# A batched matmul, scheduled by Tile or written engine by engine with its own semaphores

## The chip, the cores and the metric

The kernel runs on one core of one Trainium2 chip. The metric is the device time of one execution in microseconds (us).

The profile lists the instructions of five engines. In the kernel before, PE multiplies (768 matmuls, 189.9 us busy), DVE (VectorE) casts (48 casts, 83.1 us), ACT (ScalarE) empties the accumulators (64 copies, 64.9 us), SP (SyncE) issues the transfers (49 of them), and POOL (GpSimd) does nothing of note (0.2 us). The transfers stand in one queue, whose packets take 98.5% of the time of the 16 DMA engines that the page counts.

## The reference

```python
batch, m, k, n = 16, 512, 768, 1024
x: (batch, k, m) float32      y: (batch, k, n) float32
out = einsum('bkm,bkn->bmn', x, y)      # (16, 512, 1024) float32
```

Per batch 1.57 MB of x and 3.15 MB of y are read and 2.10 MB are written: 6.82 MB, of which nothing can be spared.

## The kernel before

It is written in Tile: pools of rotating buffers, and Tile places every wait. Three things matter here: the order in which SP issues transfers, the two rotating buffers of each input, and the last y, which comes in two halves.

```python
    xs_pool = ctx.enter_context(tc.tile_pool(name="xs_pool", bufs=2))
    ys_pool = ctx.enter_context(tc.tile_pool(name="ys_pool", bufs=2))
    ...
    o_pool = ctx.enter_context(tc.tile_pool(name="o_pool", bufs=5))
    LAG = 4
    ...
        for b in range(B):
            ...
            halves = 2 if b == B - 1 else 1
            nc.sync.dma_start(xs[:], x_v[b])
            for h in range(halves):
                ks = slice(h * KT // halves, (h + 1) * KT // halves)
                nc.sync.dma_start(ys[:, ks], y_v[b, :, ks])
            if b >= LAG:
                store(b - LAG)
            ...
            nc.vector.tensor_copy(x_sb[:], xs[:])
            for h in range(2):
                ks = slice(h * KH, (h + 1) * KH)
                nc.vector.tensor_copy(y_sb[:, ks], ys[:, ks])
            ...
            for h in range(halves):
                for mo in range(MT):
                    ...   # 6 matmuls for each of two accumulator halves
                    if h == halves - 1:
                        nc.scalar.copy(o_sb[:, mo]..., ps[mo][:])
        for b in sorted(o_tiles):
            store(b)
```

The store of a batch is issued four batches after its loads (`LAG`), so that in the end four older stores stand in the queue behind the last y.

Of the kernel before, what the change touches and what calls it, by code (L numbers as in the profile page):

```python
# [1 line left out]

_os.environ.setdefault("NEURON_RT_ULTRASERVER_MODE", "4")

# [1 line left out]

# [4 lines left out]


@with_exitstack
def kernel(
    ctx: ExitStack,
    tc: tile.TileContext,
    x: bass.AP,
    y: bass.AP,
    out: bass.AP,
):  # L20
    nc = tc.nc
    P = 128
    FP32 = mybir.dt.float32
    BF16 = mybir.dt.bfloat16

    B, K, M = x.shape
    _, _, N = y.shape
    KT = K // P
    MT = M // P
    NF = 512  # L30
    NT = N // NF



    x_v = x.rearrange("b (p ko) m -> b p ko m", ko=KT)
    y_v = y.rearrange("b (p ko) n -> b p ko n", ko=KT)
    o_v = out.rearrange("b (p mo) n -> b p mo n", mo=MT)

    xs_pool = ctx.enter_context(tc.tile_pool(name="xs_pool", bufs=2))
    ys_pool = ctx.enter_context(tc.tile_pool(name="ys_pool", bufs=2))  # L40
    x_pool = ctx.enter_context(tc.tile_pool(name="x_pool", bufs=2))
    y_pool = ctx.enter_context(tc.tile_pool(name="y_pool", bufs=2))
    o_pool = ctx.enter_context(tc.tile_pool(name="o_pool", bufs=5))
    psum = ctx.enter_context(tc.tile_pool(name="psum", bufs=4, space=bass.MemoryType.PSUM))
    LAG = 4
    KH = KT // 2
    o_tiles = {}

    def store(b):
        o_sb = o_tiles.pop(b)  # L50

        nc.sync.dma_start(o_v[b], o_sb[:])

    with tc.manual_schedule():
        for b in range(B):
            xs = xs_pool.tile([P, KT, M], FP32, name="xs")
            ys = ys_pool.tile([P, KT, N], FP32, name="ys")
            halves = 2 if b == B - 1 else 1
            nc.sync.dma_start(xs[:], x_v[b])  # L59
            for h in range(halves):  # L60
                ks = slice(h * KT // halves, (h + 1) * KT // halves)
                nc.sync.dma_start(ys[:, ks], y_v[b, :, ks])
            if b >= LAG:
                store(b - LAG)
            x_sb = x_pool.tile([P, KT, M], BF16, name="x_sb")
            y_sb = y_pool.tile([P, KT, N], BF16, name="y_sb")
            nc.vector.tensor_copy(x_sb[:], xs[:])  # L67
            for h in range(2):
                ks = slice(h * KH, (h + 1) * KH)
                nc.vector.tensor_copy(y_sb[:, ks], ys[:, ks])  # L70
            x_w = x_sb[:].rearrange("p k (j mo) -> p k mo j", mo=MT)
            o_sb = o_pool.tile([P, MT, N], FP32, name="o_sb")
            o_tiles[b] = o_sb
            ps = {}


            for h in range(halves):
                for mo in range(MT):
                    if h == 0:
                        ps[mo] = psum.tile([P, NT, NF], FP32, name="ps")  # L80
                    for nt in range(NT):
                        for kt in range(h * KT // halves, (h + 1) * KT // halves):
                            nc.tensor.matmul(  # L83
                                ps[mo][:, nt], x_w[:, kt, mo],
                                y_sb[:, kt, nt * NF:(nt + 1) * NF],
                                start=(kt == 0), stop=(kt == KT - 1))
                    if h == halves - 1:
                        nc.scalar.copy(o_sb[:, mo].rearrange("p (t f) -> p t f", f=NF), ps[mo][:])  # L88
        for b in sorted(o_tiles):
            store(b)  # L90


# [1 line left out]
_INS = ['x', 'y']  # L94
_OUTS = [((16, 512, 1024), 'float32')]


# [23 lines left out]
```

## Time and profile before

| | before |
|---|---|
| time, median of the runs | 262.0 us (261.9 to 262.17) |
| span of the profile | 260.4 us |
| rate over the span | 419 GB/s |
| first load issued | 0.73 us |
| last store issued | 246.03 us |

The main lines of the page and of the timeline are in the prediction below. The page's list of transfers (what it writes and reads, the issuing queue, how many, size, median time from issue to landing):

```profile
ys<-in_y_dram SPq DMA_DIRECT2D x15, 3072.0 KB, 28.1
...
xs<-in_x_dram SPq DMA_DIRECT2D x16, 1536.0 KB, 29.7
```

1.57 MB take 29.7 us to land, where 428 GB/s would need 3.7: so most of those 29.7 us are spent behind other transfers. The view of the line that closes the program (minimum, median and maximum duration in ns, then start of the first and of the last such instruction):

```profile
L116 SPq DRAIN  x3: 7/7/7, 259.7 to 260.0; - x3
...
L116 PEldq EVENT_SEMAPHORE  x2: 51/51/51, 259.9 to 260.4; - x2
```

When the last store has landed, SP joins two rounds of "all engines are done", at 259.7 and 260.0, and PE's answer to the second one, at 260.4, ends the span. This is the frame of the program; it costs 0.7 us after the last landing.

### The profile page before, as it was taken

The numbers are of one execution on the slowest core, as the hardware profiler recorded it, in microseconds if no ns is written. First come the engines' busy times: TensorE is split into PE (matmuls) and PEld (weight loads), VectorE is DVE, ScalarE is ACT, GpSimd is POOL, SyncE is SP. The second block draws the span as 40 slices with busy tenths as digits, with TensorE's granted clock in tenths as the row PEclk, the third lists the DMA queues.
The fourth block names the chain that finished last, engine by engine and source line by source line (L and its number), as shares of the span: only waits on it lengthen the run. The fifth ranks groups of instructions, "written<-read, shape, count | busy, mean of one in ns | idle before, by whom it ended". The sixth has DMA issues, their size and how long they took to land.

```text
span 260.4 us, 1815 instructions
## 1 busy us (share of the span) xinstructions
PE 189.9 (73%) x768; PEld 89.1 (34%) x768; DVE 83.1 (32%) x48; ACT 66.2 (25%) x65; POOL 0.2 (0%) x4
## 2 busy tenths in 40 slices
PE   0049999897939949598495956939789597899600
PEld 0014555453513514244142422514325233355200
DVE  0271734525222252322524214252132522252000
ACT  1003343433321313314033330412404114131600
POOL 0000000000000000000000000000000000000000
PEclk9999999999986997979899997997959869799955
DMA  7999999999999999999999999999999999999995
GB/s 276 430 427 425 451 420 436 423 386 421 439 428 430 422 433 445 418 435 422 435 436 414 452 405 448 429 415 452 413 434 426 421 447 416 427 437 422 428 435 214
DMA packets 7065, 109.18 MB, mean 419 GB/s; under 512 B 784, under 2 KB 784, under 8 KB 784
## 3 DMA queue, kind: packets, MB, share of 16 engines
q1 hardware_dynamic: 7056, 109.06, 98.5%
q8 instruction: 6, 0.10, 0.1%
q14 instruction: 3, 0.02, 0.0%
HBM read 75.50 MB, written 33.55 MB: 419 GB/s over the span
## 4 chain that ended last, share of the span: by engine, by line
DMA 74%; DVE 11%; PE 8%; ACT 0%; issue 0%; SPq 0%; DVEq 0%
DMA ys<-in_y_dram 74%; DVE y_sb L70 11%; PE ps L83 8%; ACT o_sb L88 0%; SPq L59 0%; DVEq L70 0%
## 5 line engine op out<-in xcount | busy, mean ns | idle before, releaser
L83 PE MATMUL ps<-y_sb,x_sb 128*128 128x512 bf16 x768 | 189.9, 410 | 55.1 <-DVE y_sb L70 55.1
L83 PEld LDWEIGHTS <-x_sb 128*128 128x128 bf16 x768 | 89.1, 118 | 155.3 <-issue 44.6
L88 ACT COPY o_sb<-ps 128x1024 f32<-128x1024 f32 x64 | 64.9, 1014 | 179.1 <-PE ps L83 179.1
L70 DVE CAST y_sb<-ys 128x3072 bf16<-128x3072 f32 x32 | 55.0, 1757 | 87.6 <-DMA ys<-in_y_dram 87.6
L67 DVE CAST x_sb<-xs 128x3072 bf16<-128x3072 f32 x16 | 28.2, 1760 | 66.4 <-DMA xs<-in_x_dram 65.6
L88 ACT ACT_TABLE_LOAD x1 | 1.3, 1283 | 0.7 <-PEq L105 0.7
L105 POOL MEMSET const-bfloat16-1.0<- 128x1 bf16 x1 | 0.1, 101 | 0.0
L105 POOL MEMSET const-uint8-127<- 128x1 uint8 x1 | 0.1, 101 | 0.0
L105 POOL MEMSET const-float32-0.0<- 128x1 f32 x1 | 0.1, 98 | 0.2 <-issue 0.2
L105 POOL MEMSET const-float32-1.0<- 128x1 f32 x1 | 0.1, 98 | 0.0
## 6 DMA issues: line engine op xcount, KB each, us to landing
ys<-in_y_dram SPq DMA_DIRECT2D x15, 3072.0 KB, 28.1
out_dram<-o_sb SPq DMA_DIRECT2D x16, 2048.0 KB, 32.6
xs<-in_x_dram SPq DMA_DIRECT2D x16, 1536.0 KB, 29.7
ys<-in_y_dram SPq DMA_DIRECT2D x2, 1536.0 KB, 26.1
```

The costliest lines, as they stand in the source:

```text
L67: nc.vector.tensor_copy(x_sb[:], xs[:])
L70: nc.vector.tensor_copy(y_sb[:, ks], ys[:, ks])
L83: nc.tensor.matmul(ps[mo][:, nt], x_w[:, kt, mo], y_sb[:, kt, nt * NF:(nt + 1) * NF], start=(kt == 0), stop=(kt == KT - 1))
L88: nc.scalar.copy(o_sb[:, mo].rearrange("p (t f) -> p t f", f=NF), ps[mo][:])
L105: nc = _bacc.Bacc("TRN2", target_bir_lowering=False, num_devices=1)
```

## The change

The intent: the same order of work, but with each engine's program written out by hand and with semaphores of its own, in the hope that fewer and cheaper waits than Tile's give a faster kernel. It is not quite the same order: the two waits in front of a batch's loads (for the x cast, and for the y casts) are joined into one, and the halves of the last y are gone. Tile's context still stands around it (`tile_critical`, and a `Block` inside). The core of the diff, cuts marked:

```diff
-    xs_pool = ctx.enter_context(tc.tile_pool(name="xs_pool", bufs=2))
... (all pools go)
+    ctx.enter_context(tc.tile_critical())
... (buffers, one semaphore for each input and output buffer)
+    cast = ec(nc.semaphore("cast"))
+    ready = ec(nc.semaphore("ready"))
+    room = ec(nc.semaphore("room"))
+    groups = ec(nc.semaphore("groups"))
+    outs = ec(nc.semaphore("outs"))
+    block = ec(nc.Block())
+    @block.sync
+    def _(sync):
+        def store(b):
+            sync.wait_ge(outs, b + 1)
+            sync.dma_start(o_v[b], ob[b % NO][:]).then_inc(so[b % NO], 16)
         for b in range(B):
-            halves = 2 if b == B - 1 else 1
-            nc.sync.dma_start(xs[:], x_v[b])
-            for h in range(halves):
-                ks = slice(h * KT // halves, (h + 1) * KT // halves)
-                nc.sync.dma_start(ys[:, ks], y_v[b, :, ks])
+            i = b % 2
+            if b >= 2:
+                sync.wait_ge(cast, b - 1)
+            sync.dma_start(xs[i][:], x_v[b]).then_inc(sx[i], 16)
+            sync.dma_start(ys[i][:], y_v[b]).then_inc(sy[i], 16)
             if b >= LAG:
                 store(b - LAG)
...
+            nc.vector.tensor_copy(xb[i][:], xs[i][:]).then_inc(ready, 1)
...
+            vector.drain().then_inc(cast, 1)
+    def batch(tensor, i, first):
+        tensor.wait_ge(ready, 2).then_inc(ready, -2)
+        for mo in range(MT):
+            tensor.wait_ge(room, 1).then_inc(room, -1)
...
+                    if mo == 0 and nt == 0 and kt == KH:
+                        tensor.wait_ge(ready, 1).then_inc(ready, -1)
```

More of the change, by code (lines that the diff above doesn't have):

```diff
@@ L37 @@
     o_v = out.rearrange("b (p mo) n -> b p mo n", mo=MT)
-    xs_pool = ctx.enter_context(tc.tile_pool(name="xs_pool", bufs=2))
-    ys_pool = ctx.enter_context(tc.tile_pool(name="ys_pool", bufs=2))
-    x_pool = ctx.enter_context(tc.tile_pool(name="x_pool", bufs=2))
-    y_pool = ctx.enter_context(tc.tile_pool(name="y_pool", bufs=2))
-    o_pool = ctx.enter_context(tc.tile_pool(name="o_pool", bufs=5))
-    psum = ctx.enter_context(tc.tile_pool(name="psum", bufs=4, space=bass.MemoryType.PSUM))
@@ L45 @@
     LAG = 4
+    NO = 5
     KH = KT // 2
-    o_tiles = {}
-    def store(b):
-        o_sb = o_tiles.pop(b)
-        nc.sync.dma_start(o_v[b], o_sb[:])
-    with tc.manual_schedule():
-        for b in range(B):
-            xs = xs_pool.tile([P, KT, M], FP32, name="xs")
-            ys = ys_pool.tile([P, KT, N], FP32, name="ys")
-            halves = 2 if b == B - 1 else 1
-            nc.sync.dma_start(xs[:], x_v[b])
-            for h in range(halves):
-                ks = slice(h * KT // halves, (h + 1) * KT // halves)
-                nc.sync.dma_start(ys[:, ks], y_v[b, :, ks])
+    GP = NT * NF
@@ new lines @@
+    ctx.enter_context(tc.tile_critical())
+    ec = ctx.enter_context
+    xs = [ec(nc.sbuf_tensor(f"xs{i}", [P, KT, M], FP32)) for i in range(2)]
+    ys = [ec(nc.sbuf_tensor(f"ys{i}", [P, KT, N], FP32)) for i in range(2)]
+    xb = [ec(nc.sbuf_tensor(f"xb{i}", [P, KT, M], BF16)) for i in range(2)]
+    yb = [ec(nc.sbuf_tensor(f"yb{i}", [P, KT, N], BF16)) for i in range(2)]
+    ob = [ec(nc.sbuf_tensor(f"ob{i}", [P, MT, N], FP32)) for i in range(NO)]
+    ps = [ec(nc.psum_tensor(f"ps{i}", [P, NT, NF], FP32)) for i in range(MT)]
@@ new lines @@
+    sx = [ec(nc.semaphore(f"sx{i}")) for i in range(2)]
+    sy = [ec(nc.semaphore(f"sy{i}")) for i in range(2)]
+    so = [ec(nc.semaphore(f"so{i}")) for i in range(NO)]
+    cast = ec(nc.semaphore("cast"))
[9 more added lines that the diff above has]
+            sync.dma_start(o_v[b], ob[b % NO][:]).then_inc(so[b % NO], 16)
+        for b in range(B):
+            i = b % 2
[3 more added lines that the diff above has]
+            sync.dma_start(ys[i][:], y_v[b]).then_inc(sy[i], 16)
@@ L63, with _ @@
             if b >= LAG:
                 store(b - LAG)
-            x_sb = x_pool.tile([P, KT, M], BF16, name="x_sb")
-            y_sb = y_pool.tile([P, KT, N], BF16, name="y_sb")
-            nc.vector.tensor_copy(x_sb[:], xs[:])
+        for b in range(B - LAG, B):
+            store(b)
+        for i in range(NO):
+            sync.wait_ge(so[i], 16 * len(range(i, B, NO)))
+    @block.vector
+    def _(vector):
+        for b in range(B):
+            i = b % 2
+            n = 16 * (b // 2 + 1)
+            if b >= 2:
+                vector.wait_ge(groups, MT * (b - 1))
+            vector.wait_ge(sx[i], n)
+            nc.vector.tensor_copy(xb[i][:], xs[i][:]).then_inc(ready, 1)
+            vector.wait_ge(sy[i], n)
@@ L68 @@
             for h in range(2):
                 ks = slice(h * KH, (h + 1) * KH)
-                nc.vector.tensor_copy(y_sb[:, ks], ys[:, ks])
-            x_w = x_sb[:].rearrange("p k (j mo) -> p k mo j", mo=MT)
-            o_sb = o_pool.tile([P, MT, N], FP32, name="o_sb")
-            o_tiles[b] = o_sb
-            ps = {}
-            for h in range(halves):
-                for mo in range(MT):
-                    if h == 0:
-                        ps[mo] = psum.tile([P, NT, NF], FP32, name="ps")
-                    for nt in range(NT):
-                        for kt in range(h * KT // halves, (h + 1) * KT // halves):
-                            nc.tensor.matmul(
-                                ps[mo][:, nt], x_w[:, kt, mo],
-                                y_sb[:, kt, nt * NF:(nt + 1) * NF],
-                                start=(kt == 0), stop=(kt == KT - 1))
-                    if h == halves - 1:
-                        nc.scalar.copy(o_sb[:, mo].rearrange("p (t f) -> p t f", f=NF), ps[mo][:])
@@ L89 @@
-        for b in sorted(o_tiles):
-            store(b)
+                nc.vector.tensor_copy(yb[i][:, ks], ys[i][:, ks]).then_inc(ready, 1)
+            vector.drain().then_inc(cast, 1)
+    def batch(tensor, i, first):
+        x_w = xb[i][:].rearrange("p k (j mo) -> p k mo j", mo=MT)
+        tensor.wait_ge(ready, 2).then_inc(ready, -2)
+        for mo in range(MT):
+            tensor.wait_ge(room, 1).then_inc(room, -1)
+            for nt in range(NT):
+                for kt in range(KT):
+                    if mo == 0 and nt == 0 and kt == KH:
+                        tensor.wait_ge(ready, 1).then_inc(ready, -1)
+                    mm = nc.tensor.matmul(
+                        ps[mo][:, nt], x_w[:, kt, mo],
+                        yb[i][:, kt, nt * NF:(nt + 1) * NF],
+                        start=(kt == 0), stop=(kt == KT - 1))
+            mm.then_inc(groups, 1)
@@ new lines, in _ @@
+    @block.tensor
+    def _(tensor):
+        for b in range(B):
+            batch(tensor, b % 2, False)
+    @block.scalar
+    def _(scalar):
+        nc.scalar.nop().then_inc(room, MT)
+        for b in range(B):
+            for mo in range(MT):
+                if mo == 0 and b >= NO:
+                    scalar.wait_ge(so[b % NO], 16 * (b // NO))
+                scalar.wait_ge(groups, MT * b + mo + 1)
+                nc.scalar.copy(ob[b % NO][:, mo].rearrange("p (t f) -> p t f", f=NF),
+                               ps[mo][:]).then_inc(room, 1)
+            scalar.drain().then_inc(outs, 1)
```

## The prediction

> **What bounds the kernel now.** I read the page first. Its parts 2, 3 and 5 give these lines (part 2 is the span in 40 slices):
>
> ```profile
> span 260.4 us, 1815 instructions
> ...
> DMA  7999999999999999999999999999999999999995
> GB/s 276 430 427 425 451 420 436 423 386 421 439 428 430 422 433 445 418 435 422 435 436 414 452 405 448 429 415 452 413 434 426 421 447 416 427 437 422 428 435 214
> ...
> HBM read 75.50 MB, written 33.55 MB: 419 GB/s over the span
> ...
> L83 PE MATMUL ps<-y_sb,x_sb 128*128 128x512 bf16 x768 | 189.9, 410 | 55.1 <-DVE y_sb L70 55.1
> ```
>
> The reader is to see that only the first and the last slice of the DMA row are below 9 tenths. 109.05 MB (75.50 read, 33.55 written) at the 428 GB/s of the middle of the run is 254.8 us; the other 5.6 us of the span are the ramp at the start, the uneven end, and the program's frame. PE waits 55.1 us in total for casts, so it has room. The change moves not one byte less.
>
> The second view is the timeline of the queue that issues the transfers, in one steady period of 15.8 us, with one batch of loads and one store in each:
>
> ```profile
> 182.47 0.33 SPq L59 DMA_DIRECT2D xs<-in_x_dram  x1
> 191.38 0.33 SPq L62 DMA_DIRECT2D ys<-in_y_dram  x1
> 191.76 0.43 SPq L52 DMA_DIRECT2D out_dram<-o_sb  x1
> 198.28 0.33 SPq L59 DMA_DIRECT2D xs<-in_x_dram  x1
> ```
>
> x of batch 14 is issued at 182.47, y at 191.38, the store of batch 10 right after it. When does that y land? The chain of waits says it in its last pieces:
>
> ```profile
> 191.38 28.07 DMA ys<-in_y_dram
> 219.46 0.03 issue
> ...
> 219.55 3.44 DVE y_sb L70 x2
> 222.99 0.04 issue
> 223.03 21.93 PE ps L83 x93
> 244.97 0.02 issue
> 244.99 1.01 ACT o_sb L88
> ```
>
> 28.07 us at 428 GB/s is 12.0 MB, and this y is only 3.15 MB. So at the moment of issue some 8.9 MB of earlier requests still stood ahead of it: the queue is never near empty, and it serves in order. The landings fit this order: the timeline has the cast of x 13 start at 196.50, of y 13 at 203.74, of x 14 at 212.30, of y 14 at 219.55. From y 13 to x 14 are 8.56 us, which at 428 GB/s is 3.66 MB: the 2.10 MB of store 9 and the 1.57 MB of x 14. From x 14 to y 14 are 7.25 us, 3.10 MB: y 14 alone. The end of the kernel is therefore set by this one queue and not by the chain through PE, although the chain view names DVE and PE: after the last eviction at 246.0 the transfers run on. The table of windows shows how long:
>
> ```profile
> 246.00:254.00 8.00, 0.00 (x0) 0.00 (x0) 0.00 (x0) 0.00 (x0) 0.00 (x0) 0.57 1.00 428
> 254.00:258.00 4.00, 0.00 (x0) 0.00 (x0) 0.00 (x0) 0.00 (x0) 0.00 (x0) 0.50 0.77 332
> 258.00:261.00 3.00, 0.00 (x0) 0.00 (x0) 0.00 (x0) 0.00 (x0) 0.00 (x0) 0.50 0.04 16
> ```
>
> The columns are the stretch, its length, the busy time of PE, weight load, DVE, ACT and POOL, the clock, the DMA share and GB/s. After 246.0 no engine computes, and 4.8 MB are still moved, of which the last store is 2.10 MB. The older 2.7 MB take about 6.3 us.
>
> [...] after PE idled at 191.2 the weight loads come every 0.43 us until 195.6 and then about twice as fast. [...] The trace has the two y casts back to back, 3.43 us for two of 1.757 us with a semaphore on each[...].
>
> **The change part by part.**
>
> (1) *Waits before loads.* Before, x of batch b+2 was issued when the x cast of b ended, y when the second y cast of b ended. After, both wait for `cast`, that is for the end of all three casts. x is issued 8.9 us later (182.47 moves to about 191.4). Still ahead of it in the queue at 191.4: the rest of store 8 and x 13 (landed by 196.5), y 13 (landed by 203.7) and store 9 (about 208.6), that is 17 us of transfers. The order in the queue, x, y, store, stays the same. Cost: 0. At the start: x 2 is issued at 18.1 and not 9.1, while y 1 is still coming (its cast starts at 25.62). The queue holds 7.5 us of work. Cost: 0.
>
> (2) *Semaphore instructions.* PE gets 6 waits with a decrement per batch, 96 in all; an event-semaphore instruction takes 17 ns on SP and 51 ns on PE in the rows of the frame's line. 96 by 51 ns is 4.9 us at worst, spread over PE's 55.1 us of idle time. DVE and ACT get one drain a batch; 16 of each at tens of ns, beside 87.6 and 179.1 us of waiting. Between PE's end and the store: one more drain, about 0.05 us. Cost on the path: 0.1 us.
>
> (3) *The last y in one piece.* Before, the last y came in halves, cast at 231.77 and 235.35, and PE did the first half's 24 matmuls of all four groups in between. After, nothing of y can be cast before the whole has landed, at 235.35. The first cast is done at 237.1, the second at 238.9. PE does 3 matmuls, waits for the second, then does 45. Warm at 0.216 us (9.87 us for 45 in the timeline at 52.05 is 0.219) that is 238.9 + 9.8 = 248.7. PE will have idled from 234.6 to 237.1, and such pauses (2.5 to 2.7 us) were followed by a cold start in this trace: 45 matmuls in 12.08 us at 191.41 and 12.70 at 207.22. Cold: 251.0 to 251.6. Add the last eviction, 1.01 us, and 0.1 for the hand-over: the last store is issued at 249.8 (warm) to 252.7 (cold), against 246.03 before, so 4 to 7 us later. But the queue without this store has work until about 246.0 + 6.3 = 252.3, and its slowest engines, which set the end, until about 253.7 (the last data moved near 258.6; one store takes 4.9 us). The first data come about 0.6 to 1 us after an issue (issue at 0.73, first data in the second microsecond). So data of the last store would start at 250.6 to 253.7 against a need at 252.3 to 253.7. Exposed: 0 warm, 0 to 1.4 cold. I take 0.3 us.
>
> (4) *The frame.* The program still stands inside the frame of before, with its barriers, and gets a section and a block with an entry and an exit for all engines. At the end of before, from the last landing (259.7) to the end (260.4), two rounds of drains and semaphores take about 0.35 us each, and the entry round about the same (first issue at 0.73). One more entry and one more exit: 0.7 us. This is an estimate from those rows.
>
> Sum: 262.0 + 0 + 0.1 + 0.3 + 0.7 = 263.1.
>
> **The rivals.**
>
> *A: the queue runs dry.* If the single wait in front of x and y came late enough, the DMA row would show gaps in each period. Against it: 17 us of backlog at the time of the later issue. For it: only the start, where 7.5 us are left. Were I wrong on the in-order service, up to a few us per batch would go, and 270 or more would come out. I give this 2 in 100.
>
> *B: the last y's single piece is fully exposed.* If the older stores had drained sooner, the 4 to 7 us later store would show in full: 266 to 269. For it: the larger chain and the cold clock. Against it: 6.3 us of older stores behind the last eviction. Partly exposed, by 1 to 2 us, is well possible; in full hardly.
>
> *C: leaner waits make it faster.* Fewer semaphore steps between cast, matmul and eviction could save some tenths per batch. Against it: that time is idle time of engines that the DMA queue outlasts. It can't bring the queue's 254.8 us down. Gain at most the frame's few tenths, if the entry by hand were shorter: 261.5.
>
> *D: the transfers themselves run at another rate*, because the buffers lie elsewhere or because requests arrive in bunches of three. The same sizes and 12288 and 24576 bytes per partition remain, and nothing in the trace speaks for it. A percent either way would be 2.6 us.
>
> **Range and chances.** The centre is 263.0. Below: no cost of frame and tail at all, 262.0, and a little for C, 261.4. Above: a cold PE at the end (1.4) and a frame twice as dear (1.4) make 264.9. A 2% change would be 256.8 or 267.3: the first needs fewer bytes or a faster queue, the second rival A or B. Chances: 0.01 faster, 0.95 same, 0.04 slower.
>
> **What would show it.** Step 1: the slices of the DMA row stay at 9, and y still comes some 15.8 us apart; x goes to landing in about 21 us rather than 29.7. Step 2: PE's busy time stays near 190 us. Step 3: the last eviction ends near 250 to 252.6 rather than 246.0, and the DMA share shows no hole, or one of a microsecond, before the last store. Step 4: the first load is issued later than 0.73, and the time between the last landing and the end of the span grows. The prediction is wrong if slices in the middle fall under 9, if the bytes differ, or if a hole of over 3 us stands ahead of the last store.

The sum came to 263.1 (262.0 + 0 + 0.1 + 0.3 + 0.7), and each term is worked out or estimated from the traces of the kernel before. Where the text gives an input without its source, the trace of before has this:

- A matmul of 0.216 us, called warm: evictions 2.59 us apart with 12 matmuls to each (198.35, 200.94, 203.53). Warm and cold are told apart by the granted clock in the windows: 1.00 from 143.7 to 153.6, where 45 matmuls took 9.87 us, and 0.50 from 191.4 to 195.6, at the head of 45 that took 12.08.
- A drain, "tens of ns": 14 ns on ACT and 19 on DVE at the shortest in the rows of L116.
- The last data, "near 258.6": 259.16 by the records of the packets.
- The "some tenths per batch" of rival C are a guess. The pieces of the chain between the landing of y 14, its casts, the matmuls and the eviction (219.46 to 219.55, 222.99, 244.97) add up to 0.15 us. The "few us per batch" of rival A are a guess as well.

## The result

262.91 us (262.81 to 263.11, 4 runs) against 262.0 us (261.9 to 262.17, 4 runs). The ratio is 1.0035, with a 95% interval of 1.0018 to 1.0052. Ratios here are the mean time of one kernel's fast runs over that of the other kernel's fast runs of the same rounds, so not quite the ratio of the medians. Executions over 1.5% slower than the fastest of the same kernel are left out of the means. The kernel is slower by 0.9 us, and that is clear of the noise.

The page of the changed kernel, the lines that answer to those of before:

```profile
span 261.3 us, 1921 instructions
...
DMA  7999999999999999999999999999999999999994
GB/s 271 429 440 410 440 416 448 425 371 424 435 426 431 423 430 451 401 449 421 438 430 420 444 423 435 416 430 446 416 440 423 429 436 426 437 430 426 429 401 196
...
L105 PE MATMUL ps<-yb,xb 128*128 128x512 bf16 x768 | 188.3, 407 | 62.2 <-PEq L100 55.8
...
xs<-in_x_dram SPq DMA_DIRECT2D x16, 1536.0 KB, 20.8
```

The DMA row (its digits are the busy share of the 16 DMA engines in 40 slices of the span) is as full as it was. The landing of an x has fallen from 29.7 to 20.8 us, by 8.9 us, because it is issued later and lands at the same time. PE waits 7.1 us more, and nothing comes of it.

The end, in the table of windows of the changed kernel (stretch, length, busy time of PE, weight load, DVE, ACT, POOL, clock, DMA share, GB/s):

```profile
246.00:254.00 8.00, 4.58 (x22) 2.15 (x19) 0.00 (x0) 2.48 (x3) 0.00 (x0) 1.00 0.97 412
254.00:258.00 4.00, 0.00 (x0) 0.00 (x0) 0.00 (x0) 0.00 (x0) 0.00 (x0) 0.73 0.86 369
258.00:262.00 4.00, 0.00 (x0) 0.00 (x0) 0.00 (x0) 0.00 (x0) 0.00 (x0) 0.50 0.05 20
```

Where no engine computed after 246.0 in the kernel before, PE and ACT still work here, and the transfers run on at nearly the same rate beside them (412 GB/s from 246 to 254, against 428). The last store is issued at 251.68. The frame, from the views of its three lines:

```profile
_compat.py:109 SPq COMPARE_BRANCH  x1: 33/33/33, 259.9 to 259.9; - x1
...
L44 PEldq DRAIN  x1: 13/13/13, 260.4 to 260.4; - x1
...
L152 PEldq EVENT_SEMAPHORE  x2: 51/51/51, 260.8 to 261.3; - x2
```

SP leaves its block at 259.9, then the block, the critical section and the context each collect the engines, and the span ends at 261.3: 1.4 us, where the kernel before needed 0.7.

A sum puts the 0.9 us in place. I took from the records of the trace the time from the first byte of data on the queue to the last one, and call what is left of the span the rest:

| kernel | span | first to last data | rest |
|---|---|---|---|
| before | 260.4 | 257.4 | 3.0 |
| changed | 261.3 | 257.5 | 3.8 |

0.8 of the 0.9 us are rest, that is the frame, and 0.1 is transfer, which is less than the scatter between profiles of the same kind (up to 0.6, below).

One reading is lost with the change. The chain of waits, which went through the whole kernel before, has only two pieces of work here (two pieces of 0.02 and 0.04 us are cut):

```profile
...
239.25 11.34 PE ps L105 x45
...
250.62 1.01 ACT ob L124
```

It covers 4.7% of the span. It goes no further back than the last 45 matmuls, and it stops at the last eviction rather than at the transfers that end the run. The DMA row and the windows do not depend on it.

### The profile page after: what moved, and what is told of

It reads as the page before. It is cut to its first block, busy times and chain, and to the rows that moved or that the text cites. A ratio compares the mean times of both kernels' runs of the same rounds, so it can differ in the third digit from the quotient of the medians.

```text
span 261.3 us, 1921 instructions
## 1 busy us (share of the span) xinstructions
PE 188.3 (72%) x768; PEld 87.1 (33%) x768; DVE 83.0 (32%) x48; ACT 66.2 (25%) x65; POOL 0.2 (0%) x4
## 5 line engine op out<-in xcount | busy, mean ns | idle before, releaser
L105 PE MATMUL ps<-yb,xb 128*128 128x512 bf16 x768 | 188.3, 407 | 62.2 <-PEq L100 55.8
L105 PEld LDWEIGHTS ps<-yb,xb 128*128 128x128 bf16 x768 | 87.1, 117 | 163.0 <-issue 97.9
L124 ACT COPY ob<-ps 128x1024 f32<-128x1024 f32 x64 | 64.9, 1014 | 184.5 <-PE ps L105 184.5
L93 DVE CAST yb<-ys 128x3072 bf16<-128x3072 f32 x32 | 54.9, 1757 | 89.6 <-DMA ys<-in_y_dram 89.6
L89 DVE CAST xb<-xs 128x3072 bf16<-128x3072 f32 x16 | 28.2, 1760 | 66.5 <-DMA xs<-in_x_dram 66.5
## 6 DMA issues: line engine op xcount, KB each, us to landing
xs<-in_x_dram SPq DMA_DIRECT2D x16, 1536.0 KB, 20.8
```

What stands on the lines that cost most here:

```text
L89: nc.vector.tensor_copy(xb[i][:], xs[i][:]).then_inc(ready, 1)
L93: nc.vector.tensor_copy(yb[i][:, ks], ys[i][:, ks]).then_inc(ready, 1)
L105: mm = nc.tensor.matmul(ps[mo][:, nt], x_w[:, kt, mo], yb[i][:, kt, nt * NF:(nt + 1) * NF], start=(kt == 0), stop=(kt == KT - 1))
L124: nc.scalar.copy(ob[b % NO][:, mo].rearrange("p (t f) -> p t f", f=NF), ps[mo][:]).then_inc(room, 1)
```

## The experiments

The theory: the queue of transfers bounds both kernels and is never short of work; the 0.9 us are the frame. Rival 1: the 0.9 us are the last y in one piece. Rival 2: the later issue of x costs a little in each batch. The same sum for all runs (two profiles of like kernels differ by up to 0.6 us in their transfers, so the column tells only larger differences):

| kernel | median us | ratio to before, 95% | first to last data | rest |
|---|---|---|---|---|
| changed, last y in halves | 262.99 | 1.0028 (1.0016 to 1.0040) | 257.6 | 3.7 |
| before, last y in one piece | 261.9 | 0.9995 (0.9983 to 1.0007) | 257.2 | 2.9 |
| changed, second block | 263.23 | 1.0040 (1.0028 to 1.0052) | 256.9 | 4.1 |
| changed, no Tile context | 261.5 | 0.9977 (0.9965 to 0.9989) | 257.2 | 2.5 |
| changed, halves and no context | 261.8 | 0.9990 (0.9976 to 1.0003) | 257.0 | 2.5 |
| changed, x early | 262.94 | 1.0031 (1.0018 to 1.0043) | 257.1 | 3.8 |
| changed, loads 6 us later | 262.83 | 1.0030 (1.0012 to 1.0048) | 257.1 | 3.8 |
| changed, loads 11 us later (3 fast runs) | 266.69 | 1.0167 (1.0139 to 1.0195) | 261.8 | 3.8 |
| changed, loads one batch later | 298.12 | 1.1373 (1.1356 to 1.1389) | 292.6 | 3.7 |
| changed, stores 3 behind | 265.93 | 1.0135 (1.0119 to 1.0151) | 260.6 | 3.7 |
| before, stores 3 behind | 262.31 | 1.0006 (0.9993 to 1.0018) | 257.6 | 3.0 |
| changed, stores 2 behind | 270.05 | 1.0302 (1.0287 to 1.0316) | 264.6 | 3.7 |

All gave correct results. The rest follows what stands around the work, and nothing else that was changed: 2.9 to 3.0 with Tile's own end, 3.7 to 3.8 with context, section and block, 4.1 with one more block, 2.5 with the block alone.

### The frame: taken away, and made larger

```diff
-    ctx.enter_context(tc.tile_critical())
...
-    with _tile.TileContext(nc) as tc:
-        tile_einsum_matmul_transpose_kernel(tc, *args)
+    tile_einsum_matmul_transpose_kernel(types.SimpleNamespace(nc=nc), *args)
```

> The changed kernel with its block alone, outside of the Tile context and its critical section. Theory (frame): the stretch from the last landing to the end falls from 1.4 us to about 0.5, the first load goes out near 0.8, 262.0 or a little under. Rival (tail): 262.8 to 262.9.

261.5 us, half a microsecond lower than expected: 0.2% under the kernel before and 0.6% under the changed kernel by their ratios. The first load goes out at 0.73, and from SP's leaving of its block (259.4) to the end of the span (259.7) is under 0.4 us:

```profile
_compat.py:109 SPq COMPARE_BRANCH  x1: 33/33/33, 259.4 to 259.4; - x1
...
_compat.py:109 PEldq EVENT_SEMAPHORE  x1: 51/51/51, 259.7 to 259.7; - x1
```

The rest fell by 1.3 us. The frame is not only enough to explain the 0.9 us; without it the hand-written program is the faster of the two. It still has the last y in one piece and the joined wait, which speaks against both rivals as a cause.

```diff
+    dummy = ec(nc.semaphore("dummy"))
+    with nc.Block() as first:
+        @first.sync
+        def _(sync):
+            sync.nop().then_inc(dummy, 1)
     block = ec(nc.Block())
```

> The changed kernel with one more block in front of it, which holds one empty instruction: one more entry and exit barrier. Theory (frame): the first load goes out later by 0.3 to 0.6 us than 0.94, and the time is 263.2 to 263.6. Rival (the frame costs nothing, the tail does): 262.9.

The trace shows what was expected of it: the first load at 1.29 and not 0.94, 0.35 us for one more block, and 0.3 us more of rest. The time alone would not have told it: its ratio of 1.0040 and the changed kernel's 1.0035 have overlapping intervals.

### The last y: halves given back, and taken from the kernel before

```diff
+            halves = 2 if b == B - 1 else 1
+            for h in range(halves):
+                ks = slice(h * KT // halves, (h + 1) * KT // halves)
+                sync.dma_start(ys[i][:, ks], y_v[b, :, ks]).then_inc(sy[i] if h == 0 else sl, 16)
... (DVE and PE follow, for the last batch only)
```

> The changed kernel with the last y in two transfers again, and PE doing the last batch half by half. Theory (the 0.9 us lie in the frame, 0.2 at the entry and 0.7 at the exit; the later last store is hidden behind older stores): 262.7 to 262.9, no gain over 262.9, although the last store goes out near 246.3 in place of 251.7. Rival (the 0.9 us are the exposed tail): back to 262.0.

The last store goes out at 245.4 in place of 251.7, and the time is 262.99: the ratios, 1.0028 and 1.0035, do not differ by more than their intervals. 6.3 us earlier at the end of the chain through PE buy 0.2 us or nothing; the two intervals together leave room for half a microsecond.

```diff
-            halves = 2 if b == B - 1 else 1
+            halves = 1
```

> The kernel before with the last y in one transfer, nothing else. Theory: the last store goes out near 251.5 and not 246.0, and the time stays 262.0 to 262.2. Rival (exposed tail): 262.9.

The last store goes out at 250.5 in place of 246.03, and the time is 261.9. So the halves hid nothing that was not hidden by the older stores. Its interval allows 0.2 us of loss at most. Both runs, from both sides, go against rival 1.

### How much the older stores hide: stores three and two batches behind

If the older stores are what hides the late end of PE, then fewer of them must lay it bare, and by an amount that can be worked out.

```diff
-    LAG = 4
+    LAG = 3
```

> The changed kernel with stores three batches behind the loads in place of four. One store fewer stands behind the last y: it lands near 240.2, and three older stores (6.3 MB, 14.7 us at 428 GB/s) end near 254.9. The last store needs 16.0 us after the landing (235.7 to 251.7 in the changed kernel), so it goes out near 256.5. Theory (in-order queue, the tail was hidden with little to spare): a hole of about 2 us in the transfers, 264 to 265.5. Rival (the queue is not in order, or the tail does not matter): 262.9.

The casts of the last y start at 240.44, the last store goes out at 256.68: both as worked out. The windows of this run (columns as above):

```profile
250.00:252.00 2.00, 2.00 (x11) 1.06 (x10) 0.00 (x0) 1.02 (x1) 0.00 (x0) 1.00 0.96 410
252.00:257.00 5.00, 3.57 (x17) 1.66 (x15) 0.00 (x0) 2.03 (x2) 0.00 (x0) 1.00 0.12 52
257.00:264.00 7.00, 0.00 (x0) 0.00 (x0) 0.00 (x0) 0.00 (x0) 0.00 (x0) 0.55 0.71 300
```

Here is the hole: for 5 us the DMA engines are busy 12% of the time while PE works. The time is 265.93, 0.4 above the range. The expectation had the older stores end near 254.9; in the trace most DMA engines are out of work by 252 and the last by 254 (windows of 1 us: a share of 0.35 from 252, 0.27 from 253, 0.00 from 254).

> The kernel before with stores three batches behind. Its last store needs only 10.7 us after the last y (235.4 to 246.0), so it goes out near 250.9, ahead of 254.9. Theory: no hole, 262.0. If it slows as much as the changed kernel does, the halves are not what hides the tail.

The same edit in the kernel before: the last store at 251.5, no hole, 262.31, ratio 1.0006. So here, and only here, the halves seem to earn their place. The two runs differ in their waits and frame too, and none with three stores behind exchanges the halves alone.

> The changed kernel with stores two batches behind: last y lands near 245.2, two older stores end near 255.0, the last store goes out near 261.3. Theory: a hole of some 6.5 us, 268.5 to 270. Rival (tail does not matter): 262.9.

270.05 us, at the upper end of the range. In the windows the transfers stand still while PE ends:

```profile
250.00:255.00 5.00, 5.00 (x23) 2.54 (x22) 0.00 (x0) 1.65 (x2) 0.00 (x0) 0.94 0.48 203
255.00:260.00 5.00, 4.50 (x21) 2.15 (x19) 0.00 (x0) 1.84 (x3) 0.00 (x0) 1.00 0.00 0
```

In the changed kernel, with four stores behind, the cover is used up almost to the end: its last store goes out at 251.68, and in the two microseconds from 251 to 253 the rate is 328 and 295 GB/s. That is no hole yet.

### The wait before the loads: undone, and made later

```diff
             if b >= 2:
-                sync.wait_ge(cast, b - 1)
+                sync.wait_ge(xcast, b - 1)
             sync.dma_start(xs[i][:], x_v[b]).then_inc(sx[i], 16)
+            if b >= 2:
+                sync.wait_ge(cast, b - 1)
... (a semaphore xcast, raised by one more drain on DVE after the x cast)
```

> The changed kernel with the wait in front of x undone: x is issued when the x cast of two batches before is done, as in the kernel before. Theory: x goes out 8.9 us earlier, to landing grows from 21 to 30 us, and the time stays 262.9. Rival (the joint wait costs): 262.0 to 262.5.

262.94. The landing of x takes 29.7 us again, as in the kernel before, and the time is that of the changed kernel. Rival 2 is out.

The next three make the wait later, from batch 6 on, to see how far the free backlog goes. In the order in which they ran:

```diff
                 sync.wait_ge(cast, b - 1)
+            if b >= 6:
+                sync.wait_ge(groups, MT * (b - 1))
```

> The changed kernel, from batch 6 on the loads wait in addition for all matmuls of the batch two before, which end some 12 us after its casts. Theory (17 us of transfers stand in the queue at the present issue): some 5 us are left, no holes, 262.9 within 0.5. Rival (the present wait already costs a little in each period, so a later one costs more): 264 or more, growing with each of the ten batches.

A miss. Three runs took 265.37 to 267.55 us, by the ratio 4.4 us over before, of which 0.9 are the frame. A fourth, 274.02, counts as slow by its time and is left out; its clock, 0.899, is hardly below the 0.903 to 0.914 of the others, so it may be the scatter of this very kernel. The loads went out 10.1 to 12.3 us after the casts. Not every batch lost. The casts of y 10, 11 and 12 (batches count from 0):

```profile
158.42 3.43 DVE L95 CAST yb<-ys 128x3072 bf16<-128x3072 f32 x2 [6.44 <-DMA ys<-in_y_dram]
...
174.22 3.43 DVE L95 CAST yb<-ys 128x3072 bf16<-128x3072 f32 x2 [5.45 <-DMA ys<-in_y_dram]
...
191.41 3.43 DVE L95 CAST yb<-ys 128x3072 bf16<-128x3072 f32 x2 [6.82 <-DMA ys<-in_y_dram]
```

From y 10 to y 11 are 15.80 us, as in the changed kernel; the loads of batch 11 were 10.1 us late. From y 11 to y 12 are 17.19; the loads of batch 12 were 12.3 us late. The ten issues part cleanly in this profile: six that were 10.1 to 11.24 us late cost nothing, four that were 11.55 to 12.3 us late cost 1.0 to 1.4 us each. What stood in the queue parts them too: issued and not yet moved, by the records of the packets, were 1.5 to 2.3 MB at the six issues and 1.0 to 1.3 MB at the four. In the lossy periods the rate falls at full or nearly full busy share, after the issue (at 174.15 for batch 12) and once more some 11 us later:

```profile
175.00:176.00 1.00, 0.00 (x0) 0.00 (x0) 1.00 (x2) 0.12 (x1) 0.00 (x0) 1.00 1.02 336
...
177.00:178.00 1.00, 0.54 (x2) 0.15 (x2) 0.65 (x1) 0.00 (x0) 0.00 (x0) 0.50 0.85 352
```

The packets themselves took longer: of the 2048 packets of y, 70 took over 1.3 us, against 23 in the changed kernel, at a median of 0.91 in both. 54 of the 70 lie in the four lossy periods, none in the other six, and 16 before all of them.

```diff
-                sync.wait_ge(cast, b - 1)
+                sync.wait_ge(cast, b if b >= 6 else b - 1)
```

> The changed kernel, from batch 6 on the loads wait for the casts of the batch one before in place of two before. At that issue only the rest of one store stands in the queue: 4.9 us less the 3.5 us of casts, 1.4 us. Theory (backlog is what makes late issue free): just at the edge, each of ten periods loses 0 to 1.5 us, so 263 to 278, with dips in the DMA row; the later wait must show more than the wait for PE does. Rival (backlog does not matter): 262.9.

Beyond the range: 298.12, 3.5 us for each of the ten batches. In this kernel y lands 15.5 us after its issue and the casts take 3.4 more before the next issue, 18.9, which is nearly the period of 19.25 us (issues at 196.60 and 215.85). The buffers, in effect, have become single. Three things were left out of my sum. The store that was to fill 1.4 us was all but moved: by the packet records 0.03 to 0.24 MB were left at the ten issues. At the start of a bunch the rate was not full at once: after the issue at 196.60 it was 139 and 270 GB/s in the two microseconds from 197, and 418 from 199. And 311 packets of y took over 1.3 us. The windows of this issue, at 196.60:

```profile
196.00:197.00 1.00, 0.93 (x3) 0.14 (x2) 0.53 (x1) 0.00 (x0) 0.00 (x0) 0.50 0.24 98
...
198.00:199.00 1.00, 1.00 (x4) 0.35 (x3) 0.00 (x0) 0.00 (x0) 0.00 (x0) 0.50 0.80 270
199.00:200.00 1.00, 1.00 (x3) 0.29 (x2) 0.00 (x0) 0.00 (x0) 0.00 (x0) 0.50 1.02 418
```

The third asks whether lateness costs in proportion or only past an edge:

```diff
                 sync.wait_ge(cast, b - 1)
+            if b >= 6:
+                sync.wait_ge(groups, MT * (b - 2) + 2)
```

> As the run that made the loads wait for all matmuls of two batches before (from batch 6 on), but for two of its four groups only, so the loads go out 5 to 8 us after the casts in place of 11 to 14. That run was expected to be free and cost 4 us in ten batches, with few idle engines and with long packets of y. If lateness is free as long as a few us of backlog stand in the queue: 262.9 within 0.4 and no long packets. If lateness costs in proportion: some 264.5 to 265.

The loads go out 4.9 to 6.8 us after the casts, 262.83 us, 24 long packets of y. In these runs there is an edge: up to 11.24 us lateness was free, from 11.55 us on it cost (the first of these three runs); 3.4 to 4.3 MB stood in the queue at the issues of this run. Why packets grow long past the edge is not settled: that the loads come when the queue has little left is common to both lossy runs, but no run took the length of the queue apart from the time of issue.

### The best of both

> Both at once: the last y in halves and no Tile context around the block. Theory: no better than leaving the context out alone, near 262.0. If the tail costs some tenths too, it is the fastest of all, 261.5 to 261.8.

261.8 us, ratio 0.9990 against 0.9977 without the halves: no gain, the intervals overlap. The version without the Tile context, 261.5 us, is the fastest, and its gain on the kernel before is half a microsecond of frame.

## Why the prediction was right

**The bound.** The queue of transfers sets the time: in both kernels only the first and the last of the 40 slices of the DMA row are below 9 tenths. This held in all runs where the queue kept its backlog: 256.9 to 257.6 us from first to last data, whatever the waits. So of the rivals, A (the queue runs dry), B (the last y fully exposed) and D (another rate of transfer) did not come.

**Part 1, the joined wait: cost 0.** Shown. The transfers moved in the order of their issue: in the kernel before, x 13, y 13, store 9, x 14 and y 14 have their first data at 189.0, 192.7, 200.0, 204.8 and 208.5 and their last at 196.0, 203.2, 208.1, 211.7 and 219.0. x goes out 8.9 us later and lands when it did (20.8 against 29.7 us); giving the early issue back changes nothing. What the text got wrong beside it was how much is free. It measured the queue by landings: 17 us at the later issue, 8.9 MB ahead of y 14. But the DMA engines do not end a transfer together: from 201.5 to 203.5 in the kernel before, 69 to 96% of the packet time was already the next store, while the rest of y 13, cast from 203.74, was still coming. Counted in bytes not yet moved, the queue held 7.9 MB ahead of y 14, and 6.2 to 6.3 MB at the later issue, 14.4 to 14.8 us at 428 GB/s. Nor is all of that usable: from 11.55 us of delay on the transfers slowed. There, a later wait went with slower transfers and not only with a later issue: 70 packets of y took over 1.3 us, against 23 in the changed kernel.

**Part 2, semaphore instructions: 0.1 us.** In kind as foreseen: 96 instructions of 51 ns on PE. From the end of the first y cast to PE's first matmul it takes 0.30 us in each of the batches where PE was waiting, against 0.05 to 0.06 in the kernel before; two separate waits stand in a row there, where Tile hung one wait on the instruction itself (the view of L83 has no semaphore instruction of its own, those of L98 and L100 have 16 and 64). Behind the second y cast, with one separate wait, it is 0.14 against 0.05. PE's waiting grew from 55.1 to 62.2 us and it cost nothing. So the hand-made waits on PE are dearer, not leaner, and the gain of rival C (leaner waits) did not come; only the frame, left out, gave one.

**Part 3, the last y: 0.3 us.** The last store went out at 251.7, inside the foreseen 249.8 to 252.7; PE ran 45 matmuls in 11.33 us, between the warm 9.8 and the cold 12.1 to 12.7. Its exposure was put at 0.3; the two runs that exchange the halves show none beyond their intervals, of 0.3 to 0.5. The cover is real and small: one store fewer behind the last y laid 3 us bare. One reading was wrong: the slow weight loads, put after a pause at 191.2, are there already at 190.15 and 190.58 (0.41 and 0.43 us after the one before, granted clock 0.50 from 189.74 to 191.4), and the pause before those was 2.69 us (187.05 to 189.74); the one at 191.2 was 0.20. And a pause like that did not always bring a cold start: after 2.75 and 0.83 us of pause, 45 matmuls took 9.87 us at 143.72. The wide range from warm to cold covered this.

**Part 4, the frame: 0.7 us.** The right cause, a little larger: 0.2 us later at the start (0.73 to 0.94), 0.6 to 0.7 us longer at the end (0.7 to 1.4), 0.8 to 0.9 in all. The estimate took one round at each end, at 0.35 us each. Measured, the entry was cheaper and the end took two rounds more, for the block and for the critical section.

The mechanism was right. That the sum of 263.1 came so close to 262.91 is in part luck: the tail was put 0.3 too high and the frame 0.1 to 0.2 too low.

## What to carry to other kernels

With a DMA row that was full from end to end, rewriting the waits between engines gained nothing here: it moved 257.4 us of transfers to 257.5. What could be moved stood before the first byte and after the last: 3.8 us in the changed kernel, 2.5 without Tile's context. Behind four older stores a chain through PE could end late for free (6.3 us later cost 0.2 us or nothing), behind three the changed kernel took 3.0 us longer; so count the stores behind the last load before splitting that load. How late an issue may come was told by the usable backlog, which an experiment found, and not by the last landing: 11.2 us were free where landings promised 17.

## What the traces showed of the hardware

- The queue. x 14 was issued ahead of y 14, and their casts start at 212.30 and 219.55, in the order of issue. How much must stand in the queue for the full rate showed in the run with the loads 11 us later: with 1.5 MB or more left at the issue (up to 11.24 us after the casts) nothing was lost, with 1.3 MB or less (11.55 us and more) 1.0 to 1.4 us per batch, and 70 packets of y took over 1.3 us in place of 23.
- The clock of PE. In the kernel before, pauses of 1.45 and 0.82 us with 0.84 us of matmuls between them, ahead of 223.03, were followed by weight loads 0.43 us apart until 226.66, at a granted clock of 0.54 (window 223.0 to 226.7). The length of the pauses alone does not decide it: 2.75 and 0.83 us of pause, with 0.84 us of matmuls between them, ahead of 143.72 were followed by 45 matmuls in 9.87 us, at a granted clock of 1.00. What decides stays open.
- Semaphores. On DVE two y casts of 1.757 us with a semaphore on each take 3.43 us together in both kernels. On PE a semaphore instruction of its own takes 51 ns (17 to 28 on SP), and two in a row put the first matmul 0.30 us after the cast, against 0.05 to 0.06 with the wait on the instruction.
- Blocks. One more block in the program, entry and exit together, put the first load 0.35 us later (1.29 against 0.94). Context, section and block together make 3.8 us of span outside of the transfers, the block alone 2.5.
